# Moving the operand splits of a fused block's first stage from GpSimd to VectorE, and reordering its first loads

## The chip, the cores and the metric

The kernel runs on one core of one Trainium2 chip. The metric is the device time of one launch in microseconds (us), taken over repeated runs; lower is better. The five engines of the core are named as the profile names them: PE (TensorE; PEld is its weight load), DVE (VectorE), ACT (ScalarE), POOL (GpSimd) and SP (SyncE, which here only issues DMAs).

## What is computed

Two blocks of a sequence model on 1024 tokens of width 1024, all in float32. The first block, which the change concerns, reads

```python
z = x @ w_in[layer]
u_a, v_a, g_a, x_b, g_b, q_x, g_x = jnp.split(z, SPLITS, axis=-1)
y_a = spatial_gating(jax.nn.gelu(u_a), jax.nn.gelu(v_a), ...)
y_b = s5_branch(x_b, ...)
y_x = memory_cross_attention(q_x, mem, xa_w_k[layer], xa_w_v[layer])
y = jnp.concatenate([y_a * silu(g_a), y_b * silu(g_b), y_x * silu(g_x)], axis=-1)
x = layer_norm(DN_ALPHA * x + y @ w_out[layer], ...)
```

(`silu` stands for `jax.nn.silu`; arguments are cut to "..."). The second block has a gated linear recurrence, a differential attention, a second memory attention and a mixture of 32 experts; its code is not touched.

## The kernel before, in words

**Exact products.** Every float32 operand of a product is split into a high part, which `self.split` (L168) lets ACT round off (L154), and a low part, which is the operand less its high part, a `tensor_tensor` (L166) on DVE unless the call names another engine. `mm3` (L172) then makes three products of each pair: high by high (L174), and the two mixed ones (L175, L176). The PE can begin a low product only when the subtraction is through.

**The start.** `block1` (L452) first loads `w_gx` and the eight row tiles `xraw` of x transposed (L492), 128x1024 each, and splits them into `xh` and `xl` (L493). The tiles are loaded into six raw buffers; the seventh and eighth wait for the buffers of the third and fourth. The splits of the third and sixth tile (k = 2 and 5) make their low part on POOL, the other six on DVE. Then come the weights `w_xb`. The products that use them are named after their PSUM tiles: `pj` for `w_gx` and the other dense products (`dense`, L502; 48 matmuls of 512 columns each for a chunk of weights), and `pu` for `w_xb` (`inputs`, L541; 192 matmuls of 256 columns). `pu` has two PSUM buffers, each emptied by ACT into `U` after 48 matmuls.

**Weights.** The local function `weights` (L471) loads a 128x1024 chunk and splits it, with the low part on POOL (`eng=nc.gpsimd`) except where a call says otherwise. All further chunks of the block go through it: `w_gb`, `w_u`, `w_ga`, `w_qx`, `w_v`, `xa_w_k`, `xa_w_v`.

**Side by side.** After the start, `merge` (L71) interleaves two lanes and a filler: `left` (the S5 branch, L556, four units `u` in a long chain of small DVE, ACT and PE steps, then half of the gating), `attend` (the memory attention, L717, then the other half), and `dense`, whose products fill in. The S5 branch needs parameters computed from `cols` by `params` (L263), a chain of some 150 tiny DVE operations with a few ACT table functions in it; two of the steps are powers on POOL (L203). In each unit the chunk sums `pst` are turned (`ra`, `rb`), scanned (`gs`), turned back (`hu`, `hv`) and split into `h`, which the product `py` reads.

**Who sets the order.** A scheduler places each instruction into its engine's queue before launch, by priorities and an estimate of times; at run time every engine goes through its queue in order and waits on semaphores. `tc.high_priority` raises a stretch: 3 for x, 4 for `params`, 2 for `inputs`, in units of `URGENT`. SP's DMAs wait in order too.

**Zeros and small stores.** Four tiles of the S5 matrices (`Gh`, `Gl`, `Bh`, `Bl`, L926) and four of the attention (`kph`, `kpl`, `vph`, `vpl`, L725) are zeroed on POOL. Four stores of a zero strip `pad` to DRAM (`kd`, L929) are issued on SP.

Of the kernel before, what the change touches and what calls it, by code (L numbers as in the profile page):

```python
# [11 lines left out]
F32 = mybir.dt.float32  # L12
# [16 lines left out]
BLK = 96                    # tokens of a block of an expert  # L29
NB = -(-1024 // BLK)        # blocks that one expert can have  # L30
NY = 3
N0 = 2                          # gated outputs of the first branch that go under the attention
CT = 8                          # tokens of a chunk of the S5 states
NRA, NRB, NRX = 6, 6, 1                 # buffers of the expert weights
OVAT = 8                        # expert beside which the further blocks are listed
LIM = 78                        # chunks of expert weights after which fewer buffers take them
EMPTY = 2048                    # the token of an empty row, beyond all
NOV = 2048 // BLK + 1       # more than the blocks beyond the first ones
# [32 lines left out]
def merge(tc, lanes, fill, made):  # L71
    """emits the lanes side by side: each moves its own clock on by its pace with every step, and the one
    that is behind comes next; the clock is the priority too. A lane yields None, a new place for its
    clock, the name of work of the last lane that it needs, or a condition that another lane will fulfil.
    The last lane only has products that fill in; what takes them out of PSUM, the functions that it
    yields, goes first."""
# [3 lines left out]
    late = []  # L80
# [49 lines left out]
class Model:  # L130
# [50 lines left out]
    def gelu2(self, out, ps, pool, shape, tag):  # L181
        """out = 2 * gelu(ps)"""
        q = pool.tile(shape, F32, name=tag + "q", tag=tag + "q")
        self.act(q, ps, AF.Square, scale=GC0)
        self.stt(q, q, 1.0, ps, OP.add, OP.mult)
        self.act(q, q, AF.Tanh, scale=GC1)
        self.stt(out, q, 1.0, ps, OP.add, OP.mult)

    def exp_small(self, out, x, pool, w, name):
        """accurate exp of a small tile [128, w]"""  # L190
# [24 lines left out]
    def sincos(self, s, c, r, pool, shape, name):  # L215
        """r in [-pi, pi]"""
# [20 lines left out]
    # ------------------------------------------------------------------  # L237
    def setup(self):
# [13 lines left out]
        # half biases for sigmoids made of tanh  # L252
# [4 lines left out]
        # residents that live into the second block  # L257
# [5 lines left out]
    def params(self, P):  # L263
        """S5 and rope tables, softplus of the LRU parameter, lambda of the differential attention;
        yields between its steps"""
# [8 lines left out]
        # S5: step, lambda * step  # L274
# [14 lines left out]
        # rotation of one step and of its doublings, up to half of all tokens  # L289
# [17 lines left out]
        # expm1(a) = 2 tanh(a/2) / (1 - tanh(a/2))  # L307
# [11 lines left out]
        # lambda to the powers 0 .. CT, and what a chunk leaves of a state's modulus  # L319
# [4 lines left out]
        for lev in range(4):  # L324
# [5 lines left out]
            if 0 < lev < 3:  # L330
                # the powers up to n times this one
# [11 lines left out]
        # f = (lambda_bar - 1) / lambda  # L343
# [13 lines left out]
        # b_bar = f * b  # L357
# [11 lines left out]
    def params2(self, P):  # L369
        nc, A = self.nc, self.A  # L370
        t = lambda k, w=8: P.tile([128, w], F32, name="par2_" + k)
        # rope angles
# [12 lines left out]
        # softplus(-lambda) of the LRU  # L385
# [19 lines left out]
        # lambda of the differential attention  # L405
# [11 lines left out]
    def s5_tables(self, x, y, tb, u):  # L417
        """cos(CT theta c), sin(CT theta c) of the chunks c, of two state tiles"""
# [16 lines left out]
        # ends with the last doubling  # L435

    # ------------------------------------------------------------------
    # first block
    # ------------------------------------------------------------------
# [12 lines left out]
    def block1(self):  # L452
# [18 lines left out]
        def weights(src, shape, tag, bufs=2, eng=nc.gpsimd):  # L471
# [10 lines left out]
        # x transposed, in two parts  # L482
        xh = X.tile([128, 8, 1024], F32R, name="xh")
        xl = X.tile([128, 8, 1024], F32R, name="xl")
        with tc.high_priority(3 * URGENT):
            w_gx = weights(A["w_gx"][0], [128, 8, 128], "d", 2, None)
            for k in range(8):
                if 4 <= k < 6:
                    raw = W.tile([128, 1024], F32, name="xraw", tag="wr", bufs=2)
                else:  # L490
                    raw = S5.tile([128, 1024], F32, name="xraw", tag=("u0", "u1", "k", "yt")[k % 4])
                nc.sync.dma_start(out=raw, in_=A["xT"][k])  # L492
                self.split(xh[:, k], xl[:, k], raw, nc.gpsimd if k % 3 == 2 else None)  # L493
            w_xb = [chw(A["w_xb"][j], [128, 4, 256]) for j in range(2)]

        def group(ps, ws, h):
            """one product of 512 tokens, whole"""
# [27 lines left out]
        def store_y(k, t0, y, n):  # L525
            """n token tiles of channel tile k"""
# [4 lines left out]
        # ---- S5, in chunks of CT tokens: token CT c + t is place t of chunk c. Within a chunk the outputs  # L531
        # are a matrix times the inputs; the states go from chunk to chunk ----
        U = [S5.tile([128, 8, CT, 16], F32, name="U", tag=f"u{ct}") for ct in range(2)]
        # matrices with blocks of zeros that stay: states to outputs, inputs to states
# [6 lines left out]
        def inputs():  # L541
            """x_b with the chunks on the partitions; the places backwards"""
# [13 lines left out]
        def s5():  # L556
            yield from self.params2(P)
            parp.__exit__(None, None, None)
            for u in range(4):
# [6 lines left out]
                def times(m, n, sign):  # L566
                    """m lambda^k, k < n; sign is that of the second part of m"""
# [13 lines left out]
                # states to outputs: c lambda^k  # L581
# [5 lines left out]
                # inputs to outputs: c lambda^k b, k < CT, with zeros before; every place's row is a window of it  # L587
# [16 lines left out]
                # inputs, places and channels on the partitions  # L604
# [6 lines left out]
                # what a chunk adds to the states  # L611
# [15 lines left out]
                # turned back, the states decay by a real factor  # L627
# [22 lines left out]
                # the states before each chunk  # L650
# [14 lines left out]
                # 2 gelu  # L665
# [12 lines left out]
                if u % 2:  # L678
                    # back to channels on the partitions
# [8 lines left out]
            # y_b = y * sigmoid(glu) * silu(g_b); y comes doubled  # L688
# [28 lines left out]
        def attend():  # L717
# [6 lines left out]
            for t in (kph, kpl, vph, vpl):  # L724
                nc.gpsimd.memset(t.bitcast(F32), 0.0)  # L725
# [94 lines left out]
        def gating(hp, side, wload, vps, pm_):  # L820
            """two heads of the gating; wload loads weights, vps and pm_ say where in PSUM"""
# [3 lines left out]
            # w (n g + b) + bias = (w n) g + (rows of w summed b + bias): the second part, transposed  # L825
# [74 lines left out]
        def left():  # L900
            """S5, then half of the gating in its memory, when the products that fill in are through"""
# [16 lines left out]
        with tc.high_priority(4 * URGENT):  # L918
            for _ in self.params(P):
                pass  # L920
            # b in two parts
# [3 lines left out]
        for z in Gx + BT:  # L925
            nc.gpsimd.memset(z.bitcast(F32), 0.0)  # L926
        nc.vector.memset(pad, 0.0)
        for u in range(4):
            nc.sync.dma_start(out=kd[u].rearrange("p g k n -> (p g k) n")[:, 0:7 * 16], in_=pad)  # L929
# [7 lines left out]
    # ------------------------------------------------------------------  # L937
    # w_out, residual, layer norm; then the rms norm of the second block
# [1507 lines left out]
```

## Time and profile before

| | |
|---|---|
| median of 3 runs | 2569.82 us (2568.74 to 2572.65) |
| profiled execution: span from first to last instruction | 2566.8 us |
| PE busy in it | 2402.1 us, 94% |
| DVE busy | 1774.3 us, 69% |
| ACT busy | 1246.6 us, 49% |
| POOL busy | 595.1 us, 23% |
| DMA, mean over the span | 153 GB/s |

The span is one execution under the profiler, from its first to its last instruction; for what lies around it the page has no number, and the median of the runs is 3.0 us above it. Busy shares are averages over the whole program: the first block takes roughly the first 420 us of it, the experts at the end most of the DMA traffic. An engine's wait is read from the rows that name what ended it.

### The profile page before, as it was taken

How to read it: one execution, taken by the hardware profiler on the slowest of the kernel's cores; microseconds unless marked ns; L12 is line 12 of the kernel's file. 1: busy time of each engine (PE TensorE's matmuls, PEld its weight loads, DVE VectorE, ACT ScalarE, POOL GpSimd, SP SyncE). 2: the span in 40 equal slices, each digit the busy share in tenths (PEclk: the TensorE clock that was granted, in tenths of full speed). 3: DMA queues.
4: the chain of work that ended last, by engine and by line, in shares of the span. 5: the costliest groups of instructions: out<-in, count | busy, mean ns of one | idle time of the engine just before them, and what ended most of it. 6: DMA issues, size and time to landing. Idle time of an engine off the chain costs nothing. (4 is left out here: it accounts for less than half of the span.)

```text
span 2566.8 us, 34716 instructions
## 1 busy us (share of the span) xinstructions
PE 2402.1 (94%) x13128; PEld 1993.8 (78%) x13128; DVE 1774.3 (69%) x3153; ACT 1246.6 (49%) x1854; POOL 595.1 (23%) x425
## 2 busy tenths in 40 slices
PE   6999989999999999999999989999998998999997
PEld 5988877777788889889898778888876776766665
DVE  8367576777796666666665654334557998998897
ACT  4234532344565445445445532124435776776665
POOL 4312212312222121121021010001222332233343
PEclk9999999999999999999999999999998999999999
DMA  4221245412221111101101256642246997999995
GB/s 167 63 73 63 81 140 173 134 68 78 72 85 46 50 42 54 54 30 54 61 35 40 92 193 211 200 154 91 83 197 243 366 379 284 331 372 359 353 341 200
DMA packets 101688, 392.18 MB, mean 153 GB/s; under 512 B 14352, under 2 KB 31248, under 8 KB 76944
## 3 DMA queue, kind: packets, MB, share of 16 engines
q1 hardware_dynamic: 82992, 333.31, 36.0%
q0 software_dynamic: 18528, 56.65, 7.0%
q8 instruction: 104, 1.70, 0.3%
q14 instruction: 64, 0.52, 0.1%
HBM read 338.02 MB, written 60.26 MB: 155 GB/s over the span
## 5 line engine op out<-in xcount | busy, mean ns | idle before, releaser
L154 ACT ACTIVATE wh<-raw 128x2048 fp32r<-128x2048 f32 (+2 forms) x310 | 480.0, 1557 | 322.4 <-PE pj L175 84.4
L166 DVE TENSOR_TENSOR wl<-raw,wh 128x2048 fp32r<-128x2048 f32 (+2 forms) x287 | 553.5, 1939 | 94.4 <-ACT wh L154 93.9
L174 PE MATMUL pj<-wh,xnh 128*128 128x256 f32 x768 | 222.9, 290 | 9.0 <-ACT pc L154 4.8
L2214 POOL DMA_INDIRECT out<-y,lsti x32 | 146.8, 4588 | 355.6 <-DVE y L162 351.2
L176 PE MATMUL pj<-wh,xnl 128*128 128x256 f32 x768 | 218.4, 284 | 0.0
L175 PE MATMUL pj<-wl,xnh 128*128 128x256 f32 x768 | 217.9, 284 | 0.0
L175 PE MATMUL pg<-wl,xh 128*96 128x512 f32 x512 | 205.1, 401 | 13.3 <-DVE wl L166 12.6
L176 PE MATMUL pg<-wh,xl 128*96 128x512 f32 x512 | 201.9, 395 | 0.0
L174 PE MATMUL pg<-wh,xh 128*96 128x512 f32 x512 | 200.5, 397 | 0.0
L174 PEld LDWEIGHTS pj<-wh,xnh 128*128 128x128 f32 x768 | 145.7, 190 | 11.9 <-ACT pc L154 6.7
L179 POOL TENSOR_TENSOR ss<-ss,mhalf 128x4 f32<-128x4 f32 (+1 forms) x68 | 74.3, 1093 | 315.5 <-DVE ss L163 223.5
L175 PEld LDWEIGHTS pj<-wl,xnh 128*128 128x128 f32 x768 | 146.6, 191 | 0.0
L176 PEld LDWEIGHTS pj<-wh,xnl 128*128 128x128 f32 x768 | 145.6, 190 | 0.0
L154 ACT ACTIVATE e<-sc,st,ss 128x1024 f32<-128x1024 f32 (+7 forms) x128 | 105.6, 828 | 67.8 <-DVE st L158 50.5
L175 PEld LDWEIGHTS pg<-wl,xh 128*96 128x96 f32 x512 | 82.8, 162 | 55.8 <-DVE wl L166 23.2
L174 PEld LDWEIGHTS pg<-wh,xh 128*96 128x96 f32 x512 | 83.0, 162 | 37.3 <-ACT wh L154 2.2
L176 PEld LDWEIGHTS pg<-wh,xl 128*96 128x96 f32 x512 | 83.2, 162 | 33.3 <-DVE xl L166 0.2
L174 PE MATMUL pj<-xnh,wh 128*128 128x512 f32 x256 | 103.3, 404 | 5.6 <-ACT wh L154 5.6
L174 PE MATMUL pg<-xnh,wh 128*128 128x512 f32 x256 | 103.7, 405 | 0.0
L175 PE MATMUL pg<-xnl,wh 128*128 128x512 f32 x256 | 102.6, 401 | 0.0
L176 PE MATMUL pg<-xnh,wl 128*128 128x512 f32 x256 | 102.4, 400 | 0.0
L175 PE MATMUL pj<-xnl,wh 128*128 128x512 f32 x256 | 102.2, 400 | 0.0
(1001 smaller groups left out, 6673.1 us busy)
## 6 DMA issues: line engine op xcount, KB each, us to landing
raw<-in_w_gu SPq DMA_DIRECT2D x128, 1024.0 KB, 8.7
raw<-in_w_dn SPq DMA_DIRECT2D x64, 1024.0 KB, 9.6
raw<-in_w_out SPq DMA_DIRECT2D x16, 512.0 KB, 4.0
ta<-tg POOLq DMA_DIRECT2D x32, 256.0 KB, 2.7
t<-ta SPq DMA_DIRECT2D x14, 512.0 KB, 4.7
raw<-in_w_ga SPq DMA_DIRECT2D x12, 512.0 KB, 3.7
raw<-in_w_v SPq DMA_DIRECT2D x12, 512.0 KB, 3.5
xraw<-in_xT SPq DMA_DIRECT2D x8, 512.0 KB, 6.9
```

Of the source, the lines that this page charges most:

```text
L154: return self.nc.scalar.activation(out=out, in_=in_, func=func, **kw)
L166: return (eng or self.nc.vector).tensor_tensor(out=out, in0=a, in1=b, op=op)
L174: mm(ps, l[0], r[0], start=start, stop=False)
L175: mm(ps, l[0], r[1], start=False, stop=False)
L176: mm(ps, l[1], r[0], start=False, stop=stop)
L179: self.nc.gpsimd.tensor_tensor(out=out, in0=in_, in1=self.mhalf[:, :w], op=OP.pow)
L2214: return nc.gpsimd.indirect_dma_start(out=self.out, out_offset=bass.IndirectOffsetOnAxis(ap=u["row"], axis=0), in_=u["y"], in_offset=None, ...
```

## The change

Six edits, all in the first block; comments and descriptions that the changed file also drops do nothing.

1. `weights` splits on DVE by default, so no chunk of the block goes through POOL; neither do the third and sixth tile of x.
2. The priority of loading and splitting x rises from 3 to 5, above `params` (4).
3. x gets seven raw buffers (the seventh tile takes the place of a later dense tile, `at`); the eighth follows the first in its buffer.
4. The eight tiles of zeros are written by DVE.
5. The four stores of `pad` are issued by POOL.
6. By these priorities the scheduler places the queues anew; the order after the first block stays, apart from neighbours that change places on DVE and SP.

```diff
-        def weights(src, shape, tag, bufs=2, eng=nc.gpsimd):
+        def weights(src, shape, tag, bufs=2, eng=None):
...
-        with tc.high_priority(3 * URGENT):
-            w_gx = weights(A["w_gx"][0], [128, 8, 128], "d", 2, None)
+        with tc.high_priority(5 * URGENT):
+            w_gx = weights(A["w_gx"][0], [128, 8, 128], "d", 2)
             for k in range(8):
-                if 4 <= k < 6:
-                    raw = W.tile([128, 1024], F32, name="xraw", tag="wr", bufs=2)
-                else:
-                    raw = S5.tile([128, 1024], F32, name="xraw", tag=("u0", "u1", "k", "yt")[k % 4])
+                P_, tag, bufs = ((S5, "u0", 1), (S5, "u1", 1), (S5, "k", 1), (S5, "yt", 1),
+                                 (W, "wr", 2), (W, "wr", 2), (DN, "at", 1), (S5, "u0", 1))[k]
+                raw = P_.tile([128, 1024], F32, name="xraw", tag=tag, bufs=bufs)
                 nc.sync.dma_start(out=raw, in_=A["xT"][k])
-                self.split(xh[:, k], xl[:, k], raw, nc.gpsimd if k % 3 == 2 else None)
+                self.split(xh[:, k], xl[:, k], raw)
...
             for t in (kph, kpl, vph, vpl):
-                nc.gpsimd.memset(t.bitcast(F32), 0.0)
+                nc.vector.memset(t.bitcast(F32), 0.0)
...
         for z in Gx + BT:
-            nc.gpsimd.memset(z.bitcast(F32), 0.0)
+            nc.vector.memset(z.bitcast(F32), 0.0)
         nc.vector.memset(pad, 0.0)
         for u in range(4):
-            nc.sync.dma_start(out=kd[u].rearrange("p g k n -> (p g k) n")[:, 0:7 * 16], in_=pad)
+            nc.gpsimd.dma_start(out=kd[u].rearrange("p g k n -> (p g k) n")[:, 0:7 * 16], in_=pad)
```

**The load queue at the start.** SP's queue, from its first transfer, before (`bc`, `cmat`, `dsk`, `pos` and `lq` are small tables; `raw` is a chunk of weights):

```order
L244 DMA cols<-in_cols 128x127
L270 DMA bc<-in_s5b 128x256
L272 DMA cmat<-in_s5c 128x256
L924 DMA dsk<-in_ssd 16x16
L473 DMA raw<-in_w_gx 128x1024
L492 DMA xraw<-in_xT 128x1024 x6
L929 DMA kd_181<-pad 128x112
```

and now:

```order
L244 DMA cols<-in_cols 128x127
L473 DMA raw<-in_w_gx 128x1024
L491 DMA xraw<-in_xT 128x1024 x7
L270 DMA bc<-in_s5b 128x256
L272 DMA cmat<-in_s5c 128x256
L923 DMA dsk<-in_ssd 16x16
L374 DMA pos<-in_pos 128x8
L407 DMA lq<-in_lamqk 128x256
L473 DMA raw<-in_w_gx 128x1024
L491 DMA xraw<-in_xT 128x1024
L473 DMA raw<-in_w_xb 128x1024 x2
```

The first chunk of weights and seven tiles of x now stand ahead of the small tables, the eighth behind them and behind the second `w_gx` chunk; the four `pad` stores are gone from here.

**The last x split on VectorE.** DVE's queue around the subtractions for the seventh and eighth tile, before (everything but the `xl` rows belongs to the parameters and tables of S5):

```order
L166 TENSOR_TENSOR pw<-pw,par_w_307 128x8x3
L163 TENSOR_SCALAR elk<-par_ds 128x2
L166 TENSOR_TENSOR xl<-xraw,xh 128x1024
L158 SCALAR_TENSOR_TENSOR ang<-rrk,ang 128x64
L166 TENSOR_TENSOR tb<-tab,S_249 128x2
L166 TENSOR_TENSOR tab<-tab,C_254 128x2x2
L166 TENSOR_TENSOR C_260<-C_260,par_w 128x8
L166 TENSOR_TENSOR par_w_307<-pw 128x8x3
L162 TENSOR_SCALAR elk<-elk 128x2
L166 TENSOR_TENSOR xl<-xraw,xh 128x1024
```

and now, around the eighth tile and the first `w_xb` chunk (the second `wl`):

```order
L166 TENSOR_TENSOR wl<-raw,wh 128x1024
L162 TENSOR_SCALAR ang<-par_posf 128x8 x6
L158 SCALAR_TENSOR_TENSOR esr<-esk,esr 128x8
L162 TENSOR_SCALAR ang<-par_posf 128x8 x2
L162 TENSOR_SCALAR epk<-epk 128x8
L411 TENSOR_REDUCE par_ds<-pr 128x2
L166 TENSOR_TENSOR xl<-xraw,xh 128x1024
L163 TENSOR_SCALAR rrk<-ang 128x64
L163 TENSOR_SCALAR epk<-epk 128x8
L163 TENSOR_SCALAR elk<-par_ds 128x2
L166 TENSOR_TENSOR wl<-raw,wh 128x1024
```

The last `xl` was the 120th row of the queue, behind most of the parameter chain; it is now the 44th, ahead of that chain, with some 25 tiny operations and nine large subtractions ahead of it. The zeros (thirteen rows with the smaller ones) stand at the queue's head.

**GpSimd in the S5 unit.** POOL's queue from the powers to the second unit, before (`wl` are the low parts of weights):

```order
L203 TENSOR_TENSOR epp<-two,epk 128x8
L166 TENSOR_TENSOR xl<-xraw,xh 128x1024 x2
L166 TENSOR_TENSOR wl<-raw,wh 128x1024 x3
L203 TENSOR_TENSOR elp<-two,elk 128x2
L166 TENSOR_TENSOR wl<-raw,wh 128x1024 x6
L166 TENSOR_TENSOR ra<-ra,rb 128x2x128
L166 TENSOR_TENSOR hv<-gs,tab 128x512
L166 TENSOR_TENSOR hu<-hu,hv 128x2x128
L166 TENSOR_TENSOR wl<-raw,wh 128x1024 x6
```

and now:

```order
L203 TENSOR_TENSOR epp<-two,epk 128x8
L203 TENSOR_TENSOR elp<-two,elk 128x2
L166 TENSOR_TENSOR ra<-ra,rb 128x2x128
L166 TENSOR_TENSOR hv<-gs,tab 128x512
L166 TENSOR_TENSOR hu<-hu,hv 128x2x128
L166 TENSOR_TENSOR du<-at,du 128x512
```

All large subtractions have left POOL; its three steps of an S5 unit stay. On PE the number of products is the same. In the new queue the `pst` products of the first unit are followed by 32 `pj` and 24 `pq` matmuls of 512 columns before its `py`; before it was 26 `pj` of 512 columns, 24 `pv` of 256, and eight more `pj` before the row of `py` that reads the low part of `h`. The parameter chain's ACT steps moved as well: `par_u`, the first, now stands just ahead of the first two evictions of `pu`, and the sine `C`, from which the doublings start, behind them.

## Rows read from the trace of the kernel before

**Rows 1.** Page part 1: busy time by engine, share of span.

```profile
PE 2402.1 (94%) x13128; PEld 1993.8 (78%) x13128; DVE 1774.3 (69%) x3153; ACT 1246.6 (49%) x1854; POOL 595.1 (23%) x425
```

**Rows 2.** Windows: stretch, length, busy of PE, PEld, DVE, ACT, POOL, clock, DMA.

```profile
20.00:40.00 20.00, 8.10 (x28) 6.26 (x27) 19.55 (x85) 7.86 (x9) 10.03 (x5) 0.74 0.33 115
40.00:330.00 290.00, 280.95 (x1509) 248.02 (x1509) 173.87 (x521) 119.36 (x253) 74.68 (x42) 0.98 0.25 79
```

**Rows 3.** Waits of PE, 0 to 620 us: total, times, longest.

```profile
PE pj L175 <- DVE xl L166: 10.5, 2, 10.3
PE py L176 <- DVE h L166: 4.8, 1, 4.8
```

**Rows 4.** Timeline of PE: start, length, instruction, idle before.

```profile
34.41 0.79 PE L175 MATMUL pj<-xl,wh 128*128 128x512 f32 x1 [10.29 <-DVE xl L166]
...
38.47 0.40 PE L176 MATMUL pj<-xh,wl 128*128 128x512 f32 x1
38.71 0.28 PE L175 MATMUL pu<-wl,xh 128*128 128x256 f32 x1
...
59.51 0.40 PE L174 MATMUL pu<-wh,xh 128*128 128x256 f32 x1
59.75 0.41 PE L175 MATMUL pu<-wl,xh 128*128 128x256 f32 x1
```

**Rows 5.** Timeline of DVE and POOL, 20 to 30 us; last row: `xl` by tile.

```profile
20.11 2.34 DVE L166 TENSOR_TENSOR C<-C 128x8 f32<-128x8 f32 x1
...
22.37 7.02 POOL L166 TENSOR_TENSOR wl<-raw,wh 128x1024 fp32r<-128x1024 f32 x3
...
29.49 0.15 DVE L166 TENSOR_TENSOR C<-C 128x8 f32<-128x8 f32 x1
...
L166 DVE TENSOR_TENSOR xl<-xraw,xh x6: 1210/1217/1226, 10.4 to 34.8; 128x1024 fp32r<-128x1024 f32 x6
```

**Rows 6.** Timeline of POOL and DVE, 0 to 8 us: zeros and small operations.

```profile
0.94 1.06 POOL L926 MEMSET Gh<- 128x1152 f32 x1
0.94 0.11 DVE L248 MEMSET mhalf<- 128x64 f32 x1
...
1.04 0.15 DVE L927 MEMSET pad<- 128x112 f32 x1
...
3.97 4.02 DVE L163 TENSOR_SCALAR epk<-par_al 128x8 f32<-128x8 f32 x1
...
4.33 0.95 POOL L725 MEMSET kph<- 128x1024 f32 x1
```

**Rows 7.** Timeline and DMA view, 0 to 60 us: loads (GB/s in 1.5 us slices).

```profile
1.25 0.42 SPq L270 DMA_DIRECT2D bc<-in_s5b  x1
...
11.38 1.06 ACT L154 ACTIVATE xh<-xraw 128x1024 fp32r<-128x1024 f32 x1 [0.22 <-DMA xraw<-in_xT]
...
GB/s 0 148 186 352 363 393 388 352 382 283 138 371 333 311 287 87 287 246 188 265 0 0 0 0 0 0 0 309 216 279 82 0 208 295 259 117 0 0 0 0
```

**Rows 8.** Timeline of DVE and POOL, 116 to 132 us; last row: `gt` by tile.

```profile
116.11 0.69 DVE L166 TENSOR_TENSOR ra<-pst,tab 128x512 f32<-128x512 f32 x1
...
122.79 7.41 POOL L166 TENSOR_TENSOR wl<-raw,wh 128x1024 fp32r<-128x1024 f32 x3
...
123.04 2.63 DVE L166 TENSOR_TENSOR gf<-bbar,pw 128x256 f32<-128x256 f32 x1
...
127.91 2.60 DVE L166 TENSOR_TENSOR gt<-cmat,pw 128x288 f32<-128x288 f32 x1
...
131.11 0.68 DVE L166 TENSOR_TENSOR h<-hu,h 128x508 fp32r<-128x508 f32 x1
...
L166 DVE TENSOR_TENSOR gt<-cmat,pw x8: 442/446/2602, 37.6 to 255.8; 128x288 f32<-128x288 f32 x8
```

**Rows 9.** POOL by groups, 0 to 420 us; its timeline at 97 us.

```profile
L166 POOL TENSOR_TENSOR wl<-raw,wh 128x1024 fp32r<-128x1024 f32 x23 | 55.4, 2417 | 159.3 <-ACT wh L154 147.0 <-ACT pth L154 6.7 <-DMA K<-kd 5.6
...
97.49 2.40 POOL L166 TENSOR_TENSOR wl<-raw,wh 128x1024 fp32r<-128x1024 f32 x1 [5.61 <-DMA K<-kd]
```

## The prediction, as put on record before the changed kernel ran

> **What bounds the kernel now.** I read the busy shares first, then windows of the first block, PE's waits, and the timelines of the engines that PE waited for. PE is busy 94% of the span [rows 1], and from 40 to 330 us it is busy 280.95 of 290 us [rows 2]: there it has work in its queue nearly always, so an engine beside it matters only where PE stands still. Two places stand out. Between 20 and 40 us PE is busy 8.1 us and its granted clock averages 0.74 of full speed [rows 2]; one wait of 10.3 us, for a low part of x on DVE, makes most of it [rows 3, 4]. The other is a wait of 4.8 us for `h` in the first S5 unit [rows 3].
>
> Both have one cause behind them. While POOL runs its three subtractions (7.02 us from 22.37), DVE's product of 128x8 elements takes 2.34 us; the same shape takes 0.15 us when POOL is still [rows 5]. So a split on POOL does not relieve DVE. It halts those DVE operations that meet it, about one per POOL operation of 2.4 us [rows 9], while the same subtraction on DVE takes 1.22 us [rows 5]. Before the last two x tiles DVE's queue holds the parameter chain, which crawls at this pace; the last `xl` starts at 34.8 us [rows 5], though its data had long been there.
>
> **Term 1, the start.** In the old run PE ends the first product of `w_gx` (all 48 matmuls) at the row of 38.47 and enters `pu` in earnest at 38.71 [rows 4]; from there it runs on with a pitch of 0.24 us. The question is when the new order reaches that point. Three chains compete.
>
> Loads: `w_gx` is issued where `bc` was, at 1.25 us [rows 7], and seven x tiles follow. With `cols` that is 0.06 + 8 x 0.524 = 4.26 MB ahead of and with the seventh tile, at some 0.37 MB per us (352 to 393 GB/s once the queue is full [rows 7]) 11.5 us, begun at about 3 us: the seventh lands near 14.5. Tables, second `w_gx` chunk and eighth tile are 1.45 MB more: the eighth lands near 18.5, the two `w_xb` chunks near 20 and 21.5. In the old run the third tile was there at 11.38 [rows 7].
>
> DVE: the zeros come first. Its memsets of 64 and 112 columns take 0.11 and 0.15 us [rows 6], 0.83 ns a column by their difference; two of 1152, two of 512 and four of 1024 columns come to 7,424 columns, with starts about 6.6 us. POOL took 1.06 and 0.95 us for two of these sizes [rows 6], so about 7.0 us is the other end. DVE is through with them at about 7.9 us. Then ten subtractions up to the eighth x tile (`wl`, seven `xl`, `wl`, `xl`) at 1.18 us back to back make 11.8, and some 25 tiny operations at 0.1 us 2.5: 22.2 us. That is later than the loads allow (18.5 plus 1.06 on ACT [rows 7] plus 1.2), so DVE sets it.
>
> PE: the last tile's six matmuls take 1.4 us, to 23.6. The first `w_xb` chunk is split at 22.2 + 0.3 + 1.2 = 23.7, the second some 1.5 us later, twelve `pu` matmuls (2.9 us) before it is needed. PE enters `pu` at 24.0. The gain is 38.7 - 24.0 = **14.7 us**. Bounds: if DVE cost nothing beyond the loads, 18.5 + 2.3 + 1.4 = 22.2 and 16.5 us; if zeros and tiny operations cost double, 33 instead of 24 us and 5.7 us. I take 14.7, as every price in it has its row.
>
> For the zeros two readings differ. The old row shows a `tensor_scalar` of 128x8 held 4.02 us while POOL writes zeros [rows 6]. The Trainium skill (SBUF — State Buffer, section Who interferes with whom) says that a two-input VectorE instruction does not wait for a GpSimd one that only writes, while `tensor_scalar` may, in a two-port mode. By that page the splits would not have waited for zeros on POOL and could have begun at about 6 us: moving them costs 2 us, which the 14.7 has already paid. By the row alone, read as a halt of all of DVE, moving them would be free.
>
> **Term 2, `h` of the first unit.** From `ra` at 116.11 to the end of `h` at 131.8 DVE needs 15.7 us. POOL's trio of 7.41 us stretched three of its operations to 2.63, 2.3 and 2.60 us [rows 8]; `gt` of that shape takes 0.446 when free [rows 8], so about 6.5 us are lost. Without it, and with one 1.2 us split now on DVE between them, the chain takes 10.4 us. The new PE queue puts 32 `pj` and 24 `pq` matmuls (56 x 0.23 = 12.9 us) in that place. The wait should go: **4.8 us**; bounds 0 and 4.8.
>
> **Term 3, what is handed back.** DVE takes over 25 subtractions, 25 x 1.2 = 30 us, for 60 us of POOL work that halted it [rows 5, 9]. From 40 to 330 us it is busy 174 of 290 us [rows 2], so on the sum it has room. But a subtraction in DVE's queue also makes all behind it wait for its weights. The trace cannot show that; bounds 0 and 10 us (two waits of the size of that for `h`). I take **2 us**, since DVE idles 40% of the stretch.
>
> **Costed at nothing.** The `pad` stores leave SP and cost POOL four issues; their strip is needed by the first unit's windows, some 90 us on [rows 9], and POOL has nothing but two powers near. The tables now land after x, so the parameter chain starts later: `par_u` near 30, the sine `C` behind the first evictions of `pu`, at about 43 us, against 20 before. `pu`, 192 matmuls at 0.24 [rows 4], fills PE to 24 + 46 = 70, and 20 products of `pj` and some of `pk` stand ahead of the first use of the chain, near 82. From `C` on the chain has some 150 DVE operations, most of 128x8 at 0.15 us [rows 5], a score of larger ones at 0.45 [rows 8]: at most 29 us when nothing halts it, so it is through by 72. That cover is 10 us; beyond it each microsecond is PE's. After the first block order and loads are the same, so the rest shifts as a whole.
>
> **Sum.** 14.7 + 4.8 - 2 = 17.5 us off a span of 2566.8: 2549.3. The runs' median is 3.0 us above that span, so I forecast **2552 us**.
>
> **Rivals.**
> - *Given back in the S5 chain.* The start gains, but the later parameter chain or splits at the head of DVE's queue make PE wait between 80 and 330 us. For it: `C` is 23 us later. Against: the cover above. 14.7 + 0 - 8 = 6.7 us: 2563.
> - *The start does not do what it says.* If zeros and tiny operations cost double (the bound of 33 us) and term 2 fails as well, 5.7 - 2 = 3.7 us: 2566, no change.
> - *Slower: weights halt DVE.* SP's queue has, in each S5 unit, eight loads of `K` that wait for a store to land, and weights queue behind them. In the old run POOL stood idle 5.61 us before a `wl` until a `K` load released it [rows 9], and harmed nobody. On DVE such a wait halts both lanes. Four units x 5.6 = 22.4 us, and in the units no gain at `h`: 14.7 - 22.4 gives 2578. It decides once more than 20 us of such waits reach PE; against it, the new SP order has the `w_qx` load ahead of the first `K`, and PE has filler products in each unit.
>
> **Chances.** Forecast (2545 to 2558) 0.66; given back (2558 to 2565) 0.20; no change 0.09; slower 0.05. 0.2%, about what a measurement of this kernel can tell from no change, is 5.1 us, so the first two cases count as faster, 0.86 together. The range: at best 16.5 + 4.8 with nothing handed back, 2548.5, and 3 us for what I don't see: 2545; upwards to the end of the second case, 2564.
>
> **What would show it.** Right: the `pj` wait of 10.3 us gone and `pu` entered at 22 to 26 us; no tiny DVE operation of 2 us beside a split; the `py` wait under 1 us; no new PE wait over 2 us before 330. Wrong: `pu` entered after 30 us with DVE full ahead of it, or PE waiting for `pu`'s evictions, `Gl`, `bbl` or any `wl`.

## The result, and the profile of the changed kernel

| | before | after |
|---|---|---|
| median of four runs on the same chip | 2570.82 us (2568.74 to 2572.65) | 2549.51 us (2548.57 to 2551.19) |
| span of the profiled execution | 2566.8 us | 2549.4 us |

The ratio of the times is 0.9915, with a 95% interval of 0.9903 to 0.9926: **faster by 21.3 us in the medians and by 17.4 us in the spans** of the two profiled executions. The time came out 2.5 us below the forecast, the gain in span within 0.1 us of its 17.5. The busy times on the page of the changed kernel:

```profile
PE 2400.7 (94%) x13128; PEld 1995.1 (78%) x13128; DVE 1776.6 (70%) x3186; ACT 1247.7 (49%) x1854; POOL 530.6 (21%) x396
```

PE does the same work as in [rows 1], so what went is time in which PE stood still. DVE gained only 2.3 us of busy time, though 25 subtractions of 1.2 us and 6.6 us of zeros came to it, 36.6 us together. So, as an estimate, some 34 us of what [rows 1] call busy on DVE was waiting inside an instruction.

Where PE stood still is read from windows, with the columns of [rows 2]. First two stretches of the kernel before that are not shown there:

```profile
0.00:20.00 20.00, 9.24 (x29) 6.28 (x30) 17.34 (x65) 10.06 (x15) 13.90 (x18) 1.00 0.83 287
40.00:290.00 250.00, 243.57 (x1294) 215.58 (x1294) 150.91 (x476) 98.81 (x213) 65.22 (x36) 0.99 0.23 72
```

Then the changed kernel:

```profile
0.00:20.00 20.00, 9.51 (x26) 7.06 (x27) 17.99 (x42) 11.41 (x11) 6.57 (x12) 1.00 0.88 326
20.00:40.00 20.00, 20.00 (x87) 19.17 (x85) 13.37 (x59) 7.21 (x12) 4.18 (x3) 1.00 0.66 208
40.00:290.00 250.00, 248.41 (x1355) 218.07 (x1354) 168.43 (x573) 109.66 (x238) 24.92 (x20) 1.00 0.23 69
```

PE is busy 12.2 us more in the first 40 us (0.3 in the first half, 11.9 in the second, against [rows 2]) and 4.8 us more from 40 to 290. That is 17.0 us of the 17.4. (A busy PE is not always a fast one: from 12.30 to 17.42 us it goes at about half its later pace, as the timeline shows.) The waits of PE that are left up to 620 us (total, times, longest):

```profile
PE pj L174 <- ACT xh L154: 7.7, 1, 7.7
PE pm L174 <- ACT vh L154: 6.3, 1, 6.3
...
PE pz L174 <- ACT glh L154: 3.2, 1, 3.2
...
PE pj L175 <- DVE xl L166: 2.8, 1, 2.8
PE prs L839 <- ACT wsh L154: 2.6, 2, 2.2
```

Both waits of [rows 3] are gone: nothing waits for `h`, and the 2.8 us for `xl` are the wait for the very first low part. New is that `pz`, the output gate of the S5 branch, waits 3.2 us for its weights `glh`, from 289.06 to 292.23 us.

The start, in the timelines of PE and of DVE (start, length, instruction, idle before). PE of the changed kernel:

```profile
11.71 0.80 PE L175 MATMUL pj<-xl,wh 128*128 128x512 f32 x1 [2.81 <-DVE xl L166]
12.30 0.63 PE L176 MATMUL pj<-xh,wl 128*128 128x512 f32 x1
...
17.42 0.62 PE L176 MATMUL pj<-xh,wl 128*128 128x512 f32 x1
17.85 0.42 PE L174 MATMUL pj<-xh,wh 128*128 128x512 f32 x1
18.11 0.40 PE L175 MATMUL pj<-xl,wh 128*128 128x512 f32 x1
...
25.57 0.29 PE L175 MATMUL pu<-wl,xh 128*128 128x256 f32 x1
```

DVE of the changed kernel:

```profile
8.07 0.91 DVE L724 MEMSET vpl<- 128x1024 f32 x1 [0.16 <-issue]
...
9.30 1.22 DVE L166 TENSOR_TENSOR wl<-raw,wh 128x1024 fp32r<-128x1024 f32 x1
10.44 2.35 DVE L166 TENSOR_TENSOR xl<-xraw,xh 128x1024 fp32r<-128x1024 f32 x2
...
21.43 1.21 DVE L166 TENSOR_TENSOR xl<-xraw,xh 128x1024 fp32r<-128x1024 f32 x1
```

The last `xl` starts at 21.43 instead of 34.8 us [rows 5], and PE enters `pu` in earnest at 25.57 instead of 38.71 [rows 4]. From 11.71 on PE never stands still there. And the first S5 unit on DVE:

```profile
110.38 0.69 DVE L166 TENSOR_TENSOR ra<-pst,tab 128x512 f32<-128x512 f32 x1 [0.20 <-PE pst L176]
...
118.09 0.41 DVE L166 TENSOR_TENSOR gf<-bbar,pw 128x256 f32<-128x256 f32 x1
...
119.17 0.45 DVE L166 TENSOR_TENSOR gt<-cmat,pw 128x288 f32<-128x288 f32 x1
...
119.61 0.67 DVE L166 TENSOR_TENSOR h<-hu,h 128x508 fp32r<-128x508 f32 x1
```

`gf` takes 0.41 us where [rows 8] have 2.63, `gt` 0.45 where they have 2.60; from `ra` to the end of `h` it is 9.9 us instead of 15.7.

How much of the gain reaches the end of the block, by tile (shortest, median and longest in ns, first and last start): the S5 branch's gate `pz` and the transposes `ptr` after the block, in the kernel before

```profile
L174 PE MATMUL pz<-yh,glh x8: 388/438/628, 310.7 to 321.0; 128*128 128x512 f32 x8
L951 PE MATMUL ptr<-ident,xnt x64: 270/272/446, 437.0 to 512.5; 128*128 128x128 f32 x64
```

and in the changed kernel:

```profile
L174 PE MATMUL pz<-yh,glh x8: 394/514/796, 292.2 to 301.3; 128*128 128x512 f32 x8
L950 PE MATMUL ptr<-ident,xnt x64: 270/272/448, 420.2 to 495.7; 128*128 128x128 f32 x64
```

`pz` starts 18.5 us earlier, `ptr` 16.8; the rest of the program moves with it.

### The profile page after: what moved, and what is told of

Read it like the earlier page. It is cut to its first block, busy times and chain, and to the rows that moved or that the text cites. A ratio compares the mean times of both kernels' runs of the same rounds, so it can differ in the third digit from the quotient of the medians.

```text
span 2549.4 us, 34718 instructions
## 1 busy us (share of the span) xinstructions
PE 2400.7 (94%) x13128; PEld 1995.1 (78%) x13128; DVE 1776.6 (70%) x3186; ACT 1247.7 (49%) x1854; POOL 530.6 (21%) x396
## 5 line engine op out<-in xcount | busy, mean ns | idle before, releaser
L166 DVE TENSOR_TENSOR wl<-raw,wh 128x2048 fp32r<-128x2048 f32 (+2 forms) x310 | 581.9, 1887 | 113.6 <-ACT wh L154 111.0
L175 PE MATMUL pg<-wl,xh 128*96 128x512 f32 x512 | 204.9, 400 | 13.3 <-DVE wl L166 12.6
L174 PEld LDWEIGHTS pj<-wh,xnh 128*128 128x128 f32 x768 | 145.8, 190 | 11.9 <-ACT pc L154 6.7
```

The source lines that it names most:

```text
L166: return (eng or self.nc.vector).tensor_tensor(out=out, in0=a, in1=b, op=op)
L174: mm(ps, l[0], r[0], start=start, stop=False)
L175: mm(ps, l[0], r[1], start=False, stop=False)
```

## The theory, its rivals and the experiments

**Theory of the halts:** an instruction on POOL that reads its operands from SBUF holds up a DVE instruction that reads both of its operands from SBUF, so the subtractions on POOL cost DVE, and through it PE, more than they save; taking them off POOL is the whole gain. **Rivals:** the new order of loads and the seventh buffer bring the start forward by themselves; or it is any work on POOL, or any added instruction that shifts the scheduler's order, that costs time. Each comparison below is with the kernel before on the same chip; the medians of before were 2570.0 to 2570.9 us in all of them. V means the subtraction is on VectorE, P on Pool; "rest" is all the other edits. The last columns are PE's busy time by windows and the span of the profiled execution, in us.

| weights | x | rest | median | ratio to before, 95% interval | PE busy 0 to 40 | 40 to 290 | span |
|---|---|---|---|---|---|---|---|
| P | P | old (before) | 2570.8 | | 17.3 | 243.6 | 2566.8 |
| V | P | old | 2555.6 | 0.9927 to 0.9953 | 24.2 | 249.9 | 2553.5 |
| P | V | old | 2563.9 | 0.9969 to 0.9987 | 25.1 | 243.3 | 2559.7 |
| V | V | old | 2549.5 | 0.9903 to 0.9930 | 26.9 | 250.0 | 2551.3 |
| P | P | new | 2568.5 | 0.9985 to 1.0003 | 23.0 | 243.6 | 2566.4 |
| P | V | new | 2562.2 | 0.9957 to 0.9976 | 25.4 | 243.3 | 2559.5 |
| V | V | new (after) | 2549.5 | 0.9903 to 0.9926 | 29.5 | 248.4 | 2549.4 |

**Weights back on POOL.** The changed kernel with

```diff
-        def weights(src, shape, tag, bufs=2, eng=None):
+        def weights(src, shape, tag, bufs=2, eng=nc.gpsimd):
-            w_gx = weights(A["w_gx"][0], [128, 8, 128], "d", 2)
+            w_gx = weights(A["w_gx"][0], [128, 8, 128], "d", 2, None)
```

> The changed kernel with the weights' subtractions back on POOL (x, its buffers, its priority, zeros and pad stores as changed). Halt theory (a POOL subtraction stops the DVE operations it meets): the start keeps 10 to 12 of its 13 us, since the w_xb chunks are now split one after the other in 2.4 us each and the last x subtraction can meet one; the wait for h comes back at 3 to 5 us. 2555 to 2560 us. Rival, order alone (the gain comes from where the scheduler puts things, not from the engine of the splits): within 2 us of the changed kernel, 2548 to 2552 us.

Measured: 2562.18 us, ratio 0.9967, beyond the range of the theory of the halts on the side away from the rival. PE begins with `pu` at 23.6 us, no later than in the changed kernel (24.3), but then waits 3.8 us for a `wl` that POOL makes, and for several small things after it:

```profile
PE pu L175 <- POOL wl L166: 3.8, 1, 3.8
PE pt L802 <- ACT e L154: 3.6, 3, 1.6
```

That is PE waiting for POOL itself, which makes this `wl` in 2.34 us, after another one and a power; it is not a halt of DVE. Of the 12.7 us that this kernel loses against the changed one, PE's busy time shows 4.1 in the first 40 us and 5.1 from 40 to 290.

**Weights on DVE alone.** The kernel before with the opposite edit, and nothing else of the change:

```diff
-        def weights(src, shape, tag, bufs=2, eng=nc.gpsimd):
+        def weights(src, shape, tag, bufs=2, eng=None):
```

> The kernel before with one edit: weights split on DVE. Halt theory: the trio of POOL subtractions at 22 to 29 us is gone, so the parameter chain runs through, the last x subtraction comes some 4 to 6 us earlier (three 1.2 us splits stand ahead of it instead), and the wait for h goes (4.8 us): 2559 to 2563 us. Rival, order alone: x still stands behind the parameter chain in DVE's queue, so nothing moves at the start and DVE has 28 us more to do: 2569 to 2574 us.

Measured: 2555.63 us. One default argument brings 15 of the 21 us, more than the theory had asked for. PE's wait for `xl` falls from 10.3 us [rows 3] to 4.1 though two x tiles are still POOL's: the three weights' subtractions that ran from 22.37 us [rows 5] no longer hold the parameter chain ahead of the last `xl`.

**The x tiles on DVE alone**, **all subtractions on DVE and nothing else**, and **everything but the subtractions**. The first is the kernel before with

```diff
-                self.split(xh[:, k], xl[:, k], raw, nc.gpsimd if k % 3 == 2 else None)
+                self.split(xh[:, k], xl[:, k], raw)
```

the second has this edit and the one above, the third is the changed kernel with both undone.

> The kernel before, with one edit: all eight x splits subtract on VectorE (two of them were Pool's). Theory of the halts: only two reading Pool instructions leave the program, both in the first 35 us; they free VectorE of about 2 x 2.4 us there, so pu comes 3 to 6 us earlier, and nothing changes after it: 2563 to 2568 us, much less than the weights' edit gave (2555.6). Rival, that VectorE is the bound of the start and two more subtractions of 1.18 us on it give the gain back: 2569 to 2573 us.

> The kernel before with the weights' and the x subtractions all on VectorE, and nothing else of the change (old order, six raw buffers, zeros on Pool, small stores on the load queue). Theory that the splits are the whole change: 2549 to 2552 us, as the changed kernel. Rival, that order and buffers carry the last 4 to 6 us: 2553 to 2557 us, as with the weights' edit alone (2555.6).

> The changed kernel with both kinds of subtraction back where they were (weights after the first, and two x tiles, on Pool); order, seven raw buffers, zeros on VectorE and small stores off the load queue stay. Theory that the splits are the whole change: 2567 to 2572 us, as before. Rival, that order, buffers and zeros bring TensorE into pu earlier by themselves and keep it: 2562 to 2566 us.

Measured: 2563.92, 2549.47 and 2568.48 us. On the old order the weights bring 15.1 us (2570.7 to 2555.6), the x tiles 6.1 (2570.0 to 2563.9), both together 20.5: in the medians they add up, and reach the changed kernel's time. The profiled executions do not place the x tiles' share on top of the weights: `ptr` starts at 420.5 us with the weights alone, at 422.4 with both, at 420.2 in the changed kernel, and what makes the first of these spans longer lies behind `ptr`. Priority, seventh buffer, zeros and small stores together bring 1.7 us, and the interval holds no change (0.9985 to 1.0003). So the subtractions on POOL are all of the effect that can be measured, and the rival of the order falls. That they act through halts of DVE is not in the table but in the rows.

The last of the three shows how the two engines take turns. POOL and DVE of the changed kernel with all subtractions put back, first POOL, then DVE:

```profile
10.60 9.20 POOL L166 TENSOR_TENSOR xl<-xraw,xh 128x1024 fp32r<-128x1024 f32 x2 [3.16 <-ACT xh L154]
```

```profile
10.45 2.35 DVE L166 TENSOR_TENSOR xl<-xraw,xh 128x1024 fp32r<-128x1024 f32 x2
12.72 2.39 DVE L162 TENSOR_SCALAR par_al<-cols 128x8 f32<-128x8 f32 x1
...
15.18 2.35 DVE L166 TENSOR_TENSOR xl<-xraw,xh 128x1024 fp32r<-128x1024 f32 x2
17.45 2.36 DVE L166 TENSOR_TENSOR par_al<-par_al,cols 128x8 f32<-128x8 f32 x1
```

POOL's two subtractions take 9.20 us, four times 2.3. While DVE makes two `xl` in 2.35 us, POOL's is held; when POOL's runs, the next DVE operation, 128x8 elements, lasts 2.39 us; then it is DVE's turn again. In those 9.2 us DVE alone could have made nearly eight subtractions of 1.17 us; the two engines together made six.

In that kernel PE is busy 5.6 us more than before in the first 40 us and yet the span is 0.4 us shorter; the wait of 4.8 us for `h` is back:

```profile
PE py L176 <- DVE h L166: 4.8, 1, 4.8
```

Busy is not work done here. After 2.99 us of standing still PE begins again at 39.51 us and makes 13 matmuls of 512 columns 0.43 us apart, where the kernel before has a granted clock of 1.00. From 40 to 44 us, the kernel before and then this one:

```profile
40.00:44.00 4.00, 4.00 (x18) 4.00 (x17) 4.00 (x16) 2.42 (x4) 2.62 (x1) 1.00 0.68 215
40.00:44.00 4.00, 4.00 (x11) 3.07 (x11) 4.00 (x26) 1.22 (x2) 2.16 (x1) 0.50 0.79 248
```

By the 0.23 us of a granted clock of 1.00 these 13 lose some 2.7 us (an estimate). The last `pu` starts only 2.1 us earlier than before (85.3 against 87.4), the first `ptr` 2.4 (434.6 against 437.0); the other 2.0 us lie behind `ptr`, a stretch that takes 2127.7 to 2133.0 us in the profiled executions of all these kernels.

For the other five kernels of the table the two windows tell the span within 0.6 us: weights on DVE alone 6.9 + 6.3 = 13.1 against 13.3, x alone 7.8 - 0.2 = 7.6 against 7.1, both 15.9 against 15.5, the changed kernel with weights on POOL 8.0 - 0.3 = 7.7 against 7.3, the changed kernel 17.0 against 17.4. In the seven kernels of the sections below the same sum is 1.5 to 6.2 us less than the gain in span, so the agreement in these five is in part luck.

**Ghost reads and ghost zeros.** Is it the reading, or any work on POOL? Two kernels add work to POOL after each split of weights in the changed kernel; nobody uses what the first one makes. In the first:

```diff
             self.split(hi, lo, raw, eng)
+            for q in range(2):
+                g = DN.tile([128, 448], F32, name="ghost", tag="ghost")
+                p = hi.bitcast(F32).rearrange("p a b -> p (a b)")[:, q * 448:q * 448 + 448]
+                self.tt(g, p, p, OP.subtract, nc.gpsimd)
             return hi, lo
```

in the second:

```diff
             self.split(hi, lo, raw, eng)
+            for q in range(2):
+                nc.gpsimd.memset(raw, 0.0)
             return hi, lo
```

> The changed kernel, and behind each split of weights two subtractions of 448 columns on POOL that read the high part and write a scratch tile nobody reads (about 2.4 us on POOL a chunk, as the old subtraction took); DVE's queue at the start is the same as in the changed kernel. Halt theory: DVE's two-input operations beside them stretch to about 1.2 us; the slack of PE on the last x tile is 0.7 us and on h 2.7 us, so 2 to 4 us are lost at the start and 0 to 3 at h: 2552 to 2556 us. Rival (POOL beside DVE is harmless, what hurt before was that POOL takes twice as long for a split that PE waits for): 2549 to 2551 us.

> The changed kernel with two zeroings of the raw buffer on Pool after each split of weights (one zeroing was 1.06 us in the profile before; the buffer's next load waits for them), in the place of the two ghost subtractions that cost 8.5 us. Theory that it is Pool's reading of operands that halts VectorE's SBUF-to-SBUF additions and multiplications, and that writes alone let them pass: 2549 to 2552 us, and those instructions beside a zeroing at their usual length. Rival, that any Pool work of that length beside VectorE, or the shift in the order that added instructions bring, costs the same: 2555 to 2559 us.

Measured: the kernel with the reads is 8.5 us slower than the changed one (2557.98 us, ratio 0.9952, interval 0.9939 to 0.9965), beyond the 2552 to 2556 us of the theory; the zeros cost nothing (2549.62 us, 0.9921, 0.9907 to 0.9934). Each adds 48 instructions to the same queue after the same splits, so POOL's being busy does not explain the first. The order does in part. With the reads PE enters `pu` as in the changed kernel; its waits come later: 3.0 us in `pq` until `vpl` (to 113.15 us), 1.9 for `h`, 2.8 for `ql`, 1.9 for `e`. That `vpl` is made at 112.72 us, in the changed kernel at 112.71: no halt, but a new order on PE, which has `pq` ahead of `pj` there; with the zeros PE's order there is that of the changed kernel. ACT also waits once, 5.0 us, until a ghost frees the buffer of a `wh`. So the 8.5 us are not all halt, and how much is stays open. The halts themselves are in the rows. In the first S5 unit, with ghost reads, POOL and then DVE:

```profile
121.24 7.89 POOL L166 TENSOR_TENSOR ghost<-wh 128x448 f32<-128x448 f32 x7
```

```profile
122.56 0.89 DVE L166 TENSOR_TENSOR tb<-tab,S 128x2 f32<-128x2 f32 x1
123.37 0.15 DVE L166 TENSOR_TENSOR tab<-tab,C 128x2 f32<-128x2 f32 x1
...
125.22 0.89 DVE L166 TENSOR_TENSOR tb<-tab,S 128x2 f32<-128x2 f32 x1
```

One DVE operation per ghost is held until the ghost ends, 0.89 instead of 0.15 us. With zeros, POOL and then DVE:

```profile
110.30 1.97 POOL L478 MEMSET raw<- 128x1024 f32 x2 [0.59 <-DVE wl L166]
...
113.62 1.97 POOL L478 MEMSET raw<- 128x1024 f32 x2
```

```profile
111.86 1.22 DVE L166 TENSOR_TENSOR wl<-raw,wh 128x1024 fp32r<-128x1024 f32 x1
...
113.88 1.36 DVE L641 TENSOR_TENSOR_SCAN gs<-rho,ra 128x128 f32<-128x128 f32 x4
```

The subtraction `wl` and the four scans have their usual lengths beside the zeros. In all, 49 `tensor_tensor` operations of DVE begin beside one of these 48 zeroings: 46 keep their length, and the other three stand behind a held `tensor_scalar`. This is what the Trainium skill (SBUF — State Buffer, section Who interferes with whom) states: a VectorE instruction with two SBUF inputs contends with a GpSimd one that reads, not with one that only writes. The traces agree: 0.89 instead of 0.15 us beside a ghost that reads, 1.22 us as ever for the `wl` beside zeros.

How much DVE loses can be counted from its timeline between 24 and 290 us: for each row its length less that of the shortest row of the same form in the kernels counted together, where that is over 0.3 us. Before it is 27 us in 21 rows; in the changed kernel 6 us in 10 rows, beside the S5 steps (`ra`, `hv`, `hu`, `du`) that POOL still makes. With the ghost reads it is 25 us again. With the ghost zeros the rows add up to 25 us too, but many of them stand behind a held `tensor_scalar` and overlap it; what DVE loses is some 13 us, 5 of them before 40 us, in the parameter chain, for which PE has no need yet.

**The zeros back on POOL.** The changed kernel with

```diff
-                nc.vector.memset(t.bitcast(F32), 0.0)
+                nc.gpsimd.memset(t.bitcast(F32), 0.0)
...
-            nc.vector.memset(z.bitcast(F32), 0.0)
+            nc.gpsimd.memset(z.bitcast(F32), 0.0)
```

> The changed kernel with the eight tiles of zeros back on POOL. Theory: POOL's zeros only write and don't stop a subtraction, so DVE begins its splits when the first weights are there, near 6.5 instead of 9.3 us; PE starts its run of products 2 to 3 us earlier and ends the w_gx product when the last x tile (landed at 19.4) is split: 1 to 2.5 us faster, 2547 to 2548.5 us. Rival, zeros on POOL stop all of DVE (as the 4.02 us of one small operation could be read): splits begin no earlier than before, and the tiny parameter operations are held too: 2549.5 to 2553 us.

Measured: 2550.86 us (0.9915 to 0.9941), in the rival's range and not measurably off the changed kernel. The two microseconds that the prediction worked out from the rule of the Trainium skill are not there, but the rows do not speak against the rule. POOL and DVE of this kernel:

```profile
4.30 0.95 POOL L724 MEMSET kph<- 128x1024 f32 x1
5.19 0.95 POOL L724 MEMSET kpl<- 128x1024 f32 x1
6.09 2.42 POOL L928 DMA_DIRECT2D kd<-pad  x4
```

```profile
3.93 2.23 DVE L163 TENSOR_SCALAR epk<-par_al 128x8 f32<-128x8 f32 x1
...
6.40 1.91 DVE L163 TENSOR_SCALAR epk<-epk 128x8 f32<-128x8 f32 x1
...
9.92 5.77 DVE L166 TENSOR_TENSOR xl<-xraw,xh 128x1024 fp32r<-128x1024 f32 x5
```

The `tensor_scalar` operations, with one input, are held until the second zeroing ends, and one of them again beside POOL's issuing of the `pad` stores. With DVE free of zeros the scheduler had put them ahead of the splits, so the first `xl` starts at 9.92 instead of 10.44 us: 0.5 us, not 2. The last zeros end at 10.36 us, so only the first of the five subtractions meets them, for 0.4 us; all five follow each other every 1.15 us, unheld. The `wl` before them, beside the zeros and behind a held `tensor_scalar`, took 1.61 us from 8.78.

**Priority and buffers, one at a time.** The changed kernel with `5 * URGENT` back at `3 * URGENT`, and with the old places for the last two x tiles:

```diff
-                                 (W, "wr", 2), (W, "wr", 2), (DN, "at", 1), (S5, "u0", 1))[k]
+                                 (W, "wr", 2), (W, "wr", 2), (S5, "k", 1), (S5, "yt", 1))[k]
```

> The changed kernel with the x loads and splits back at the old priority. Theory that the order at the start is set by what is ready and by the loads, hardly by this priority: 2548 to 2551.5 us. Rival, that loading x first is what brings pu forward: pu at 28 us or later and 2553 to 2558 us.

> The changed kernel with the old raw buffers of x: tiles 6 and 7 take those of tiles 2 and 3 again, so their loads wait for subtractions that end near 13 and 15 us instead of none and of tile 0's. Theory that the loads keep ahead of VectorE (the last tile landed at 19.4 us for a subtraction at 21.4): the last x part 0 to 2 us later, 2548.5 to 2552 us. Rival, that the two loads hold up the queue behind them: last x part 3 us later or more, 2553 to 2557 us.

Measured: 2546.89 us (0.9901 to 0.9928) and 2549.17 us (0.9904 to 0.9931). Neither edit is measurably worth anything once no split is on POOL. The old priority's median is the lowest of all and below the 2548 us at which its theory began, but its interval covers the changed kernel's, so it is not shown to be faster: the spans of the kernels here that differ by nothing measurable lie between 2544.1 and 2551.3 us, and each edit lets the scheduler place its neighbours anew.

**The new wait of `pz`.** The changed kernel with the gate's weights in a buffer of their own, loaded in the last S5 unit and split there; the second kernel has the old priority of x as well:

```diff
+                if u == 3:
+                    gr = S5.tile([128, 2, 256], F32, name="glr")
+                    self.ts(gr[:, 0, 0:1], C[:, 0, 1:2], 1.0, OP.mult)
+                    nc.sync.dma_start(out=gr, in_=A["glu_w"])
...
+                if u == 3:
+                    gh = S5.tile([128, 2, 2, 128], F32R, name="glh", tag="xgh")
+                    gl = S5.tile([128, 2, 2, 128], F32R, name="gll", tag="xgl")
+                    self.split(gh.rearrange("p a b c -> p a (b c)"), gl.rearrange("p a b c -> p a (b c)"), gr)
...
-            gr = S5.tile([128, 2, 256], F32, name="glr", tag="ra")
-            nc.sync.dma_start(out=gr, in_=A["glu_w"])
...
```

> The changed kernel with the weights of the first branch's output gate loaded into a buffer of their own in the last S5 unit and split before it ends, so that the new wait of TensorE for them (3.2 us near 290 us) cannot arise. Theory that this wait is handed on to the end: 2546 to 2548 us. Rival, that the gating behind it (wsh, vh) waits for other things and takes the time back: 2549 to 2551 us.

> The same edit, with the x loads at the old priority, which alone gave 2546.9 us. Theory that the wait is worth its 3 us: 2543 to 2545 us. Rival, taken back behind it: 2546 to 2548 us.

Measured: 2548.26 us (0.9902 to 0.9929) and 2551.30 us (0.9910 to 0.9937). The first lies between its two ranges, the second beyond both of its own, on the slow side; neither is measurably off the changed kernel. The wait for `glh` is gone in both, and another has its place, that of `pty` for `yt`, which was 0.7 us:

```profile
PE pty L691 <- DVE yt L158: 3.7, 1, 3.7
```

This fits the rival. A reading of it, not tested further: with the products that fill in used up by then, PE follows the S5 chain step by step, and shortening what it waits for last only shows the step before. No version tried is shown to beat the changed kernel.

## Why the prediction was right, point by point

- **What bounds the kernel: right in the main.** By the table POOL's subtractions are the whole effect. The halts of DVE behind the two waits that the prediction named are shown by the rows; PE also waited for POOL's own subtractions, 1.6 us in the kernel before (for an `xl`) and 3.8 us with the weights back on POOL, a way that the prediction did not price.
- **Term 1, the start: 14.7 forecast, 13.1 at the entry of `pu`** (38.71 to 25.57), within its bounds of 5.7 and 16.5. DVE came out as worked: the last `xl` ends at 22.6 us, forecast 22.2, although the zeros ended at 9.0 and not 7.9, since six gaps of 0.16 to 0.19 us lie between them. What was missed is PE. The step "the last tile's six matmuls" took PE to be up to date when that tile came. It was not: from 12.30 to 17.42 us its matmuls follow each other every 0.43 us, from 17.85 on every 0.23. Fourteen at the slower pace, with that of 11.71, lost 2.8 us, and PE, never idle, reached `pu` 1.6 us late.
- **Who brings term 1: only half seen.** The prediction priced the new order as a whole. By the table the subtractions alone, on the old order, bring as much in the end; order, buffers and priority shift the entry of `pu` and are given back.
- **Term 2, `h`: right.** 4.8 us forecast; the wait is gone, `h` is through at 120.3 us and its first `py` starts at 123.0, a margin of 2.7 where 2.5 had been worked out. From 40 to 290 us PE gains 4.8 us in all. The seven kernels show where that comes from: every one with weights on POOL has 243.3 to 243.6 us of busy PE there, every one with them on DVE 248.4 to 250.0. It is not `h` alone: with the x tiles on DVE and the weights on POOL, in both orders, the wait for `h` is 1.5 us, and waits for `e`, `at` and `du` stand beside it.
- **Term 3, handed back: 2 us forecast in DVE's queue before 330 us; 1.7 us found, for other reasons.** They are what lies between the 18.5 us at `pz` and the 16.8 at `ptr`; there the waits are longer for `wsh` (2.6 us against 0.5) and `vh` (6.3 against 4.7). The 3.2 us for `glh` lie ahead of `pz` and are in the 18.5 already. They break one sign of being right, no new wait of PE over 2 us before 330, and so do the 2.2 us for `wsh` at 317. No wait of PE for a `wl`, `bbl` or `Gl` appeared, and DVE's longest wait for a `K` load ahead of a `wl` is 1.9 us, to no harm, so the slower rival had no ground. But a `wl` at the head of DVE's queue did hold up what stood behind it, for a `wh` of ACT's and with the parameter chain behind:

```profile
69.64 1.23 DVE L166 TENSOR_TENSOR wl<-raw,wh 128x1024 fp32r<-128x1024 f32 x1 [6.01 <-ACT wh L154]
```

- **Costed at nothing.** No wait of PE comes from the `pad` stores or the later parameter chain; no run moves either alone. The chain was less safe than worked out: its `bbh` was ready at 77.8 us instead of 72, and `pm` read it at 82.48, so 4.7 of the 10 us of cover were left. "The rest shifts as a whole" holds: 16.8 us at `ptr`, 17.4 at the end.
- **The first rival** (gain at the start, given back in the S5 units, 2563 us) did not come. The 2562.2 us with the weights on POOL are near its number, but by another way: POOL still makes the weights, and part of the loss is at the start.
- **The offset of 3.0 us between span and median was wrong.** In the runs after it a profiled execution takes 1.7 to 2.1 us more than its span (2551.19 against 2549.4 in the changed kernel). By that the profiled execution before was about 2568.7, its fastest run, and 2.1 us under the median of 2570.8. Hence the gain in the medians is 4 us larger than in the spans, and the forecast 2.5 us too high.
- **Luck.** The terms as measured add up to 13.1 + 4.8 - 1.7 = 16.2 us, and the span fell by 17.4. That 17.5 was forecast and 17.4 came is closer than the terms were: term 1 was 1.6 us too large, and 1.2 us of the gain have no term. (The prediction ends its second case at 2565 us in one place and at 2564 in another; nothing hangs on it.)

## What to carry to other kernels

A tiny DVE operation that lasts as long as a POOL instruction beside it is the mark to look for; it means that POOL's help costs DVE time, here 2.3 us of halt for a subtraction that DVE makes in 1.2. Before moving work off DVE, ask whether it reads SBUF while DVE does two-input work: writes alone (zeros) did no harm here to subtractions, except to those that stood behind a held `tensor_scalar`. And count what an edit does to the stage in which PE follows, not to the entry of a stage: the edits that made PE busy for 5.6 us more in the first 40 us brought nothing measurable while subtractions stayed on POOL, part of it because PE then worked at half its clock.

## What the runs showed of the hardware that I had not expected

- **Turns.** Between a two-input subtraction on POOL and two-input work on DVE neither side always wins: POOL's took 4.6 us each instead of 2.4 when DVE had subtractions ready, and DVE got through two before POOL had its turn again.
- **With an operand in PSUM there was no halt.** In the kernel before, a DVE subtraction with one operand in PSUM keeps its length (`kpl` takes 0.42 to 0.43 us all four times) beside a `wl` on POOL that runs from 97.49 to 99.89 us [rows 9]:

```profile
97.72 0.42 DVE L166 TENSOR_TENSOR kpl<-pk,kph 64x256 fp32r<-64x256 f32 x1 [4.21 <-ACT kph L154]
98.06 0.27 DVE L166 TENSOR_TENSOR Bl<-pbt,Bh 128x128 fp32r<-128x128 f32 x1
```

- **A clock that the column does not show.** From 34.4 us, after 10.29 us of standing still [rows 4], PE of the kernel before made 12 matmuls in 4.29 us at a granted clock of 0.58; in the changed kernel, after 7.68 us without work, two matmuls and 2.81 us of standing still, it made 13 in 5.69 us at a granted clock of 1.00. Windows of the one and of the other:

```profile
34.40:38.70 4.30, 4.29 (x12) 3.54 (x13) 4.23 (x24) 0.26 (x1) 0.69 (x1) 0.58 0.00 0
```

```profile
11.70:17.40 5.70, 5.69 (x13) 4.47 (x14) 5.70 (x11) 3.17 (x3) 0.73 (x1) 1.00 0.96 365
```

By their pitch, 512 columns in 0.43 us, the matmuls of both stretches are at TensorE's 1.2 GHz level (in the first up to 37.99 us); from 17.85 us on, 0.23 us apart, those of the changed kernel are near the 2.4 GHz one. So the pitch of the matmuls told the level here, the column only in one of the two.
